# SSD scan: x and B turned on VectorE in blocks of 32 and carried through DRAM, and the within-chunk products of two chunks in one block

## The chip, the cores and the metric

The kernel runs on one core of a Trainium2 chip. The metric is the device time of that core for one execution, in microseconds (us); a kernel's time is the median of several runs. The engines are named as the profile names them: PE is TensorE (matmuls and transposes, with PEld for its weight loads), DVE is VectorE, ACT is ScalarE, POOL is GpSimd, and SP is the engine whose queue issues most of the transfers.

## The reference

One layer of a hybrid decoder on a sequence of S = 512 tokens with D = 1024 channels: a projection feeds a state-space mixer (SSD) and a sliding-window attention, both are merged and projected, and a SwiGLU network follows. The change lies in the SSD part alone. Cut to that part, with 4 groups of 8 heads, a head of 64 channels, a state of 128 and chunks of T = 128 tokens (names shortened):

```python
X  = (xh * dt[..., None])                      # chunk, T, group, head, 64
a_cum = cumsum(dt * a, over the chunk)
Lmat = exp(segsum(dt * a))                     # lower triangle
CB = einsum('bclgn,bcsgn->bcgls', Cc, Bc)
y_diag = einsum('bcgels,bcsgep->bclgep', Lmat * CB, X)          # within a chunk
states = einsum('bclgn,bcgel,bclgep->bcgepn', Bc, decay, X)     # what a chunk leaves
h_in   = scan over chunks: h * exp(a_cum[-1]) + states
y_off  = einsum('bclgn,bcgepn,bcgel->bclgep', Cc, h_in, exp(a_cum))
y = y_diag + y_off + d_skip * xh
y = y * silu(z);  y = y * rsqrt(mean over the group of y*y) * w  # grouped norm
```

Before it, x, B and C come from the projection by a causal convolution over four tokens and a SiLU.

## The kernel before

Activations lie with channels on the partitions and tokens along the row. So x of one group is four tiles `xs_f` of 128 channels x 512 tokens (two heads each), B and C are a tile `bc_f` each, and y of a group is `y_g`, four such tiles side by side.

*Products.* A product of the layer's weights is made in float32 precision from halves: `mm3` (L149 to L151) issues three matmuls, high x high, high x low and low x high, for each of eight slices of 128 channels, thus 24 matmuls of 128x512 into one PSUM tile `ps_mm`. A unit is such a product with its 512 KB of weights. The class `Units` loads a unit's weights into `w_raw` (four buffers, on SP's queue, L120), ACT makes the high half `w_hi` (L135) and DVE the low half `w_lo` (L136), three units ahead of the product.

*The scan.* There are 16 steps, i = 4g + c, for group g and chunk c. A step needs matmuls that depend on each other through DVE, ACT and POOL, and between them PE works on units that wait in a list, the *filler*; `fill(6.0)` issues matmuls of the list in threes until 6.0 us of them are used, and so 27 or 30 matmuls. The filler's units are the x, B, C of the next group (`x`, with the convolution of `g_xbc`: ACT L368, three DVE operations named `cacc`, L371, and the SiLU), the z of this one (`z`) and, from group 1 on, products of the layer's end. In threes of matmuls, group 0 has 80 of them, groups 1 and 2 have 112, and group 3 has 128; the slots of a group ask for some 110. Where the list is empty `fill` issues nothing; `all_done(prefix)` issues what is left of the units of that name.

The parts of a step:
- `ssd_pre(i)`: loads `L` (the cumulated sums of one group of heads, spread over 128 partitions, 512 KB) and `E` on SP, POOL masks `L` (L754), ACT puts the exponential on its eight tiles (L759). `L` has three buffers.
- `ssd_a(i)`: PE makes `ps_cb` = B C (L774), DVE multiplies `L` by it (L778, "L*cb" below). PE transposes the chunk of x, four passes into `ps_x` (L781), DVE multiplies by dt into `X` (L784). For chunks 0 to 2 PE also transposes B (`ps_bt`, L790), ACT copies it to `bt`, and POOL makes `Xd` = X times the decay (L795). For c = 0 ACT first puts D*x into `y_g`.
- `ssd_b(i)`: PE makes `ps_st` from `Xd` and `bt` (L809), the new state `h_st` follows on POOL and DVE; PE makes `ps_yo` (L825), what the state gives, DVE multiplies it by `E` to `yo`, and POOL adds that to `y_g`. After a stretch of filler PE makes `ps_yd`, from `X` and `L`, eight matmuls for the eight heads, which the profile counts as sixteen passes (L834), and DVE adds it to `y_g` (L836).
- `gate_norm(g)`, once a group is done: DVE multiplies `y_g` by z (L850), ACT squares, POOL adds up the squares (L856), ACT and DVE make the halves `sqr` (L231), PE sums over the partitions (`ps_ms`, L863), and DVE takes a reciprocal (L865).

*Who sets the order.* PE's order is the order of the code, by hand (`manual_schedule`). The instructions of the other engines are put in order by the framework's scheduler; the PSUM tiles of the scan (`ps_cb`, `ps_x`, `ps_bt`, `ps_st`, `ps_yo`, `ps_yd`) share five buffers, and those of the filler have three of their own. Each queue issues in its order: a transfer on SP that waits holds all behind it.

The functions and the loop around the change, with the profile's line numbers:

Of the kernel before, what the change touches and what calls it, by code (L numbers as in the profile page):

```python
# [11 lines left out]
F32 = mybir.dt.float32  # L12
# [50 lines left out]
def kernel(  # L63
# [89 lines left out]
    class Filler:  # L153
# [115 lines left out]
    def axt(shape, name):  # L269
        return psX.tile(shape, F32, name=name, tag="ax")  # L270
# [463 lines left out]

    z_t, y_t, yn_t, L_t, E_t, a_t, h_t = {}, {}, {}, {}, {}, {}, {}

    def ssd_pre(i):
# [19 lines left out]
        for j in range(2):  # L757
            for t in range(4):
                nc.scalar.activation(L[:, j, t], L[:, j, t], AF.Exp, bias=nac5[:, g, j, c, t:t + 1], scale=1.0)  # L759

    def ssd_a(i):

# [15 lines left out]
        nc.vector.tensor_tensor(out=Lf, in0=Lf, in1=cb.unsqueeze(1).broadcast_to([P, 8, P]), op=ALU.mult)  # L778
        ps = axt([P, 4, 2, 64], "ps_x")
        for t in range(4):  # L780
            nc.tensor.transpose(ps[:, t].rearrange("p j d -> p (j d)"), xs[t][:, cs], ident)  # L781
        X = sd.tile([P, 4, 2, 64], F32, name="X", tag="X", bufs=2)
        for j in range(2):
            nc.vector.tensor_tensor(  # L784
                out=X[:, :, j], in0=ps[:, :, j],
                in1=dt5[:, g, j, c].unsqueeze(2).broadcast_to([P, 4, 64]), op=ALU.mult)
        bt = Xd = None
        if c < NT - 1:
            ps = axt([P, P], "ps_bt")
            nc.tensor.transpose(ps, b_f[:, cs], ident)  # L790
            bt = sd.tile([P, P], F32, name="bt", tag="bt", bufs=2)
            nc.scalar.copy(out=bt, in_=ps)
            Xd = sd.tile([P, 4, 2, 64], F32, name="Xd", tag="Xd", bufs=2)
            for j in range(2):
                nc.gpsimd.tensor_tensor(  # L795
                    out=Xd[:, :, j], in0=X[:, :, j],
                    in1=dec5[:, g, j, c].unsqueeze(2).broadcast_to([P, 4, 64]), op=ALU.mult)
        a_t[i] = (X, bt, Xd)

    def ssd_b(i):  # L800

        g, c = divmod(i, NT)
        cs = slice(c * P, (c + 1) * P)
        y, c_f, L = y_t[g], xbc_t[g, 1], L_t.pop(i)
        X, bt, Xd = a_t.pop(i)
        h_prev = h_t.pop(g, None)
        if c < NT - 1:
            pss = axt([P, 4, 2, 64], "ps_st")
            nc.tensor.matmul(  # L809
                pss.rearrange("p t j d -> p (t j d)"), bt, Xd.rearrange("p t j d -> p (t j d)"),  # L810
                start=True, stop=True)
# [18 lines left out]
        yield  # L830
        psd = axt([P, 4, P], "ps_yd")
        for t in range(4):
            for j in range(2):
                nc.tensor.matmul(  # L834
                    psd[64 * j:64 * j + 64, t], X[:, t, j], L[:, j, t], start=True, stop=True)
        nc.vector.tensor_add(y[:, :, cs], y[:, :, cs], psd)  # L836
        yield
# [432 lines left out]
```

## Time and profile before

| what | value |
|---|---|
| median of 3 runs | 1028.93 us (1028.39 to 1028.96) |
| the profiled execution | 1028.11 us, of which the span is 1026.2 us |
| DVE, ACT, POOL busy | 600.5, 505.8 and 205.5 us (59%, 49%, 20%) |
| transfers | 126.56 MB, 123 GB/s over the span |
| the chain that ended last | 86% PE, 4% DVE, 3% ACT, 3% DMA |
| weights `w_raw` | 187 transfers of 512 KB, 3.5 us each to landing |
| `L` | 16 transfers of 512 KB, 5.4 us each to landing |

The span is what the profiler sees from the first instruction to the last; the execution's time is longer by what lies around it. All edits of this change lie in the scan, which runs from about 237 to 580 us of the span.

### The profile page before, as it was taken

To read this page: it belongs to the slowest core of one execution; us is meant where nothing else is said; L and a number is where in the kernel's file an instruction comes from. 1 tells how busy PE (TensorE), PEld (TensorE's weight loads), DVE (VectorE), ACT (ScalarE), POOL (GpSimd) and SP (SyncE) were. 2 spreads that over 40 slices of the span, in tenths; PEclk is the share of its full clock that TensorE was granted. 3 is DMA by queue.
4 is the path that set the end of the run, shared out by engine and by line. 5 is a ranking of instruction groups with operands and counts; after the bars stand their busy time and mean duration, and the time that the engine had idled before them with its cause. 6 is when DMAs were issued, how large, how long until landed. Compare 5 with 4: busy or idle time off the path is not lost.

```text
span 1026.2 us, 13200 instructions
## 1 busy us (share of the span) xinstructions
PE 1014.5 (99%) x5044; PEld 837.6 (82%) x5044; DVE 600.5 (59%) x835; ACT 505.8 (49%) x864; POOL 205.5 (20%) x195
## 2 busy tenths in 40 slices
PE   9999999999999999999999999999999999999997
PEld 7888888887887878888888888898888888888886
DVE  6789874534656764676664595646433333332765
ACT  6464566717666885783733542434332333322450
POOL 2011223723115113111223820390000000000000
PEclk9999999999999999999999999999999999999999
DMA  8211223544443334334322344316433333331471
GB/s 317 83 64 61 88 83 104 203 142 130 136 135 106 113 116 126 106 115 138 89 93 82 123 150 179 102 42 225 144 123 123 106 120 106 120 123 62 154 255 43
DMA packets 38799, 126.56 MB, mean 123 GB/s; under 512 B 4528, under 2 KB 5040, under 8 KB 38480
## 3 DMA queue, kind: packets, MB, share of 16 engines
q1 hardware_dynamic: 36080, 116.14, 34.7%
q0 software_dynamic: 2080, 7.47, 2.0%
q10 hardware_dynamic: 576, 2.10, 0.6%
q8 instruction: 40, 0.66, 0.2%
q14 instruction: 23, 0.19, 0.1%
HBM read 119.27 MB, written 6.42 MB: 122 GB/s over the span
## 4 chain that ended last, share of the span: by engine, by line
PE 86%; DVE 4%; ACT 3%; DMA 3%; issue 2%; POOL 1%; SPq 0%; DVEq 0%; POOLq 0%; ACTq 0%
PE ps_mm L149 13%; PE ps_mm L150 12%; PE ps_mm L151 12%; PE ps_ff L151 8%; PE ps_ff L149 8%; PE ps_ff L150 8%; PE ps_da L151 2%; PE ps_da L149 2%; PE ps_da L150 2%; DMA L<-a_d 2%; PE ps_db L151 2%; PE ps_db L150 2%; PE ps_db L149 2%; PE ps_mix L149 1%; PE ps_mix L151 1%
## 5 line engine op out<-in xcount | busy, mean ns | idle before, releaser
L135 ACT CAST w_hi<-w_raw 128x1024 fp32r<-128x1024 f32 x185 | 193.4, 1051 | 305.5 <-PE ps_ff L150 123.2
L136 DVE TENSOR_TENSOR w_lo<-w_raw,w_hi 128x1024 fp32r<-128x1024 f32 x185 | 240.5, 1305 | 154.1 <-ACT w_hi L135 151.9
L149 PE MATMUL ps_mm<-hT_hi,w_hi 128*128 128x512 f32 x504 | 203.3, 403 | 1.0 <-DVE cacc L371 1.0
L150 PE MATMUL ps_mm<-hT_lo,w_hi 128*128 128x512 f32 x504 | 196.8, 391 | 0.0
L151 PE MATMUL ps_mm<-hT_hi,w_lo 128*128 128x512 f32 x504 | 196.6, 390 | 0.0
L149 PE MATMUL ps_ff<-h2T_hi,w_hi 128*128 128x512 f32 (+1 forms) x384 | 143.2, 373 | 0.0
L150 PE MATMUL ps_ff<-h2T_lo,w_hi 128*128 128x512 f32 (+1 forms) x384 | 142.6, 371 | 0.0
L151 PE MATMUL ps_ff<-h2T_hi,w_lo 128*128 128x512 f32 (+1 forms) x384 | 142.6, 371 | 0.0
L149 PEld LDWEIGHTS ps_mm<-hT_hi,w_hi 128*128 128x128 f32 x504 | 94.7, 188 | 23.1 <-issue 5.6
L151 PEld LDWEIGHTS ps_mm<-hT_hi,w_lo 128*128 128x128 f32 x504 | 94.6, 188 | 20.3
L150 PEld LDWEIGHTS ps_mm<-hT_lo,w_hi 128*128 128x128 f32 x504 | 94.8, 188 | 18.2 <-issue 1.0
L150 PEld LDWEIGHTS ps_ff<-h2T_lo,w_hi 128*128 128x128 f32 x384 | 72.3, 188 | 12.6
L151 PEld LDWEIGHTS ps_ff<-h2T_hi,w_lo 128*128 128x128 f32 x384 | 72.3, 188 | 12.5
L149 PEld LDWEIGHTS ps_ff<-h2T_hi,w_hi 128*128 128x128 f32 x384 | 72.3, 188 | 12.4
L1117 DVE TENSOR_TENSOR sgf<-sgf,ps_ff 128x512 f32<-128x512 f32 x22 | 15.1, 685 | 68.4 <-PE ps_ff L151 68.4
L149 PE MATMUL ps_mm<-yh,w_hi 128*128 128x512 f32 x124 | 49.2, 397 | 0.0
L150 PE MATMUL ps_mm<-yl,w_hi 128*128 128x512 f32 x124 | 48.3, 390 | 0.0
L151 PE MATMUL ps_mm<-yh,w_lo 128*128 128x512 f32 x124 | 48.3, 389 | 0.0
L371 DVE SCALAR_TENSOR_TENSOR cacc<-ps_mm,pc,cacc 128x511 f32<-128x511 f32 (+2 forms) x54 | 39.9, 741 | 9.8 <-ACT cacc L368 9.2
L759 ACT ACTIVATE L<-L,nac 128x128 f32<-128x128 f32 x128 | 40.9, 391 | 6.2 <-POOL L L754 5.9
L778 DVE TENSOR_TENSOR L<-L,cb 128x1024 f32<-128x1024 f32 x16 | 21.5, 1343 | 38.4 <-ACT cb L776 21.6
L754 POOL TENSOR_SCALAR_AFFINE_SELECT L<-L 128x1024 f32<-128x1024 f32 x16 | 20.1, 1256 | 93.9 <-DMA L<-a_d 93.9
(267 smaller groups left out, 1700.2 us busy)
## 6 DMA issues: line engine op xcount, KB each, us to landing
w_raw<-in_wall_dram SPq DMA_DIRECT2D x187, 512.0 KB, 3.5
L<-a_d SPq DMA_DIRECT2D x16, 512.0 KB, 5.4
E<-e_d SPq DMA_DIRECT2D x24, 128.0 KB, 3.5
x_d<-x_sb POOLq DMA_DIRECT2D x4, 512.0 KB, 7.8
row<-x_d POOLq DMA_DIRECT2D x4, 512.0 KB, 5.1
h_d<-row POOLq DMA_DIRECT2D x4, 512.0 KB, 3.0
h_r<-h_d ACTq DMA_DIRECT2D x4, 512.0 KB, 5.4
out_dram<-y_o SPq DMA_DIRECT2D x7, 256.0 KB, 4.1
```

What stands on the lines that cost most here:

```text
L135: (copy or nc.scalar.copy)(out=hi, in_=w)
L136: self.last = (eng or nc.vector).tensor_sub(out=lo, in0=w, in1=hi.bitcast(F32))
L149: nc.tensor.matmul(ps, lh, rh, start=start, stop=False)
L150: nc.tensor.matmul(ps, lh, rl, start=False, stop=False)
L151: nc.tensor.matmul(ps, ll, rh, start=False, stop=stop)
L371: nc.vector.scalar_tensor_tensor(out=acc[:, d:], in0=ps[:, :S - d], scalar=pc[:, cw + 3 - d:cw + 4 - d], in1=acc[:, d:], op0=ALU.mult, op1 ...
L754: nc.gpsimd.affine_select(out=Lf, in_=Lf, pattern=[[0, 8], [1, P]], compare_op=ALU.is_ge, fill=-BIG, base=0, channel_multiplier=-1)
L759: nc.scalar.activation(L[:, j, t], L[:, j, t], AF.Exp, bias=nac5[:, g, j, c, t:t + 1], scale=1.0)
L778: nc.vector.tensor_tensor(out=Lf, in0=Lf, in1=cb.unsqueeze(1).broadcast_to([P, 8, P]), op=ALU.mult)
L1117: nc.vector.tensor_mul(sg, sg, pu)
```

## The change

The transposes leave PE. A new `ssd_x(i)` turns the chunk of x on DVE: one instruction turns each 32x32 block of a 128x128 piece by itself, so that the blocks still stand in their old places; four of them write `T`. The blocks are moved to their places through DRAM: one store `T` to `t_d` (SP), and four loads to `R`, each for 32 partitions (pieces of 512 bytes). For chunks 0 to 2 it does the same with B: one transpose to `Tb`, one store to `b_d`, four loads to `bt` (pieces of 128 bytes). A new `ssd_dt(i)` makes `X` = R times dt on DVE and `Xd` on POOL. `ssd_a` keeps D*x, `ps_cb` and L*cb, and loses its five transposes, ACT's copy and the rest. `ssd_x` stands two steps ahead, `ssd_dt` one. `ssd_b` makes `ps_yd` only at even chunks, for that chunk and the next in one block of 32 passes into two PSUM tiles, and both additions to `y_g` follow. `all_done` for the next group's x moves from chunk 3 to chunk 2. `T` shares three buffers with other temporaries, `R`, `Tb` and `Xd` have one each (`Xd` had two), `X` and `bt` keep two.

```diff
--- before.py
+++ after.py
@@ -234,6 +234,8 @@
     h_d = dram.tile([S, D], F32, name="h_d")
     a_d = dram.tile([P, P], F32, name="a_d")
     e_d = dram.tile([P, P], F32, name="e_d")
+    t_d = dram.tile([NG * NT, P, 4, P], F32, name="t_d")
+    b_d = dram.tile([NG * NT, P, 4, 32], F32, name="b_d")
 
 
     def xbc(g):
@@ -732,7 +734,7 @@
     er = e_d.rearrange("(g j c t) l -> g c j (t l)", g=NG, j=2, c=NT)
     dt5, dec5, cd5, nac5 = cols(dtv), cols(dec), cols(cdec), cols(nac)
 
...
 
     def ssd_pre(i):
 
@@ -758,6 +760,52 @@
             for t in range(4):
                 nc.scalar.activation(L[:, j, t], L[:, j, t], AF.Exp, bias=nac5[:, g, j, c, t:t + 1], scale=1.0)
 
+    def ssd_x(i):
+
+        g, c = divmod(i, NT)
+        cs = slice(c * P, (c + 1) * P)
+
+        T = sd.tile([P, 4, 4, 32], F32, name="T", tag="tmp", bufs=3)
+        for t in range(4):
+            nc.vector.transpose(T[:, :, t], xbc_t[g, 2 + t][:, cs])
+
+        R = sd.tile([P, 4, 4, 32], F32, name="R", tag="R", bufs=1)
+        R_t[i] = R
+        nc.sync.dma_start(out=t_d[i], in_=T.rearrange("p b t s -> p b (t s)"))
+        for b in range(4):
+            nc.sync.dma_start(
+                out=R[32 * b:32 * b + 32].rearrange("r a t s -> r a (t s)"),
+                in_=t_d[i, :, b].rearrange("(a r) x -> r a x", r=32))
+        if c < NT - 1:
+            Tb = sd.tile([P, P], F32, name="Tb", tag="Tb", bufs=1)
+            nc.vector.transpose(Tb, xbc_t[g, 0][:, cs])
+            bt = sd.tile([P, P], F32, name="bt", tag="bt", bufs=2)
+            bt_t[i] = bt
+            nc.sync.dma_start(out=b_d[i], in_=Tb.rearrange("p (b s) -> p b s", b=4))
+            for b in range(4):
+                nc.sync.dma_start(
+                    out=bt[32 * b:32 * b + 32].rearrange("r (a s) -> r a s", a=4),
+                    in_=b_d[i, :, b].rearrange("(a r) s -> r a s", r=32))
+
+    def ssd_dt(i):
+
+        g, c = divmod(i, NT)
+        R = R_t.pop(i)
+        X = sd.tile([P, 4, 2, 64], F32, name="X", tag="X", bufs=2)
+        X_t[i] = X
+        for j in range(2):
+            nc.vector.tensor_tensor(
+                out=X[:, :, j].rearrange("p t (h s) -> p t h s", h=2),
+                in0=R[:, 2 * j:2 * j + 2].rearrange("p h t s -> p t h s"),
+                in1=dt5[:, g, j, c].unsqueeze(2).unsqueeze(3).broadcast_to([P, 4, 2, 32]), op=ALU.mult)
+        if c < NT - 1:
+            Xd = sd.tile([P, 4, 2, 64], F32, name="Xd", tag="Xd", bufs=1)
+            Xd_t[i] = Xd
+            for j in range(2):
+                nc.gpsimd.tensor_tensor(
+                    out=Xd[:, :, j], in0=X[:, :, j],
+                    in1=dec5[:, g, j, c].unsqueeze(2).broadcast_to([P, 4, 64]), op=ALU.mult)
+
     def ssd_a(i):
 
         g, c = divmod(i, NT)
@@ -776,38 +824,17 @@
         nc.scalar.copy(out=cb, in_=ps)
         Lf = L.rearrange("p j t l -> p (j t) l")
         nc.vector.tensor_tensor(out=Lf, in0=Lf, in1=cb.unsqueeze(1).broadcast_to([P, 8, P]), op=ALU.mult)
-        ps = axt([P, 4, 2, 64], "ps_x")
-        for t in range(4):
-            nc.tensor.transpose(ps[:, t].rearrange("p j d -> p (j d)"), xs[t][:, cs], ident)
-        X = sd.tile([P, 4, 2, 64], F32, name="X", tag="X", bufs=2)
-        for j in range(2):
-            nc.vector.tensor_tensor(
-                out=X[:, :, j], in0=ps[:, :, j],
-                in1=dt5[:, g, j, c].unsqueeze(2).broadcast_to([P, 4, 64]), op=ALU.mult)
-        bt = Xd = None
-        if c < NT - 1:
-            ps = axt([P, P], "ps_bt")
-            nc.tensor.transpose(ps, b_f[:, cs], ident)
-            bt = sd.tile([P, P], F32, name="bt", tag="bt", bufs=2)
-            nc.scalar.copy(out=bt, in_=ps)
-            Xd = sd.tile([P, 4, 2, 64], F32, name="Xd", tag="Xd", bufs=2)
-            for j in range(2):
-                nc.gpsimd.tensor_tensor(
-                    out=Xd[:, :, j], in0=X[:, :, j],
-                    in1=dec5[:, g, j, c].unsqueeze(2).broadcast_to([P, 4, 64]), op=ALU.mult)
-        a_t[i] = (X, bt, Xd)
 
     def ssd_b(i):
 
         g, c = divmod(i, NT)
         cs = slice(c * P, (c + 1) * P)
-        y, c_f, L = y_t[g], xbc_t[g, 1], L_t.pop(i)
-        X, bt, Xd = a_t.pop(i)
+        y, c_f = y_t[g], xbc_t[g, 1]
         h_prev = h_t.pop(g, None)
         if c < NT - 1:
             pss = axt([P, 4, 2, 64], "ps_st")
             nc.tensor.matmul(
-                pss.rearrange("p t j d -> p (t j d)"), bt, Xd.rearrange("p t j d -> p (t j d)"),
+                pss.rearrange("p t j d -> p (t j d)"), bt_t.pop(i), Xd_t.pop(i).rearrange("p t j d -> p (t j d)"),
                 start=True, stop=True)
             h = sd.tile([P, 4, 2, 64], F32, name="h_st", tag="h_st", bufs=2)
             h_t[g] = h
@@ -828,12 +855,19 @@
             nc.vector.tensor_mul(yo, pso, E_t.pop(i))
             nc.gpsimd.tensor_add(y[:, :, cs], y[:, :, cs], yo)
         yield
-        psd = axt([P, 4, P], "ps_yd")
-        for t in range(4):
-            for j in range(2):
-                nc.tensor.matmul(
-                    psd[64 * j:64 * j + 64, t], X[:, t, j], L[:, j, t], start=True, stop=True)
-        nc.vector.tensor_add(y[:, :, cs], y[:, :, cs], psd)
+
+        if c % 2 == 0:
+            psd = [axt([P, 4, P], "ps_yd") for _ in range(2)]
+            for k in range(2):
+                X, L = X_t.pop(i + k), L_t.pop(i + k)
+                for t in range(4):
+                    for j in range(2):
+                        nc.tensor.matmul(
+                            psd[k][64 * j:64 * j + 64, t], X[:, t, j], L[:, j, t],
+                            start=True, stop=True)
+            for k in range(2):
+                cs = slice((c + k) * P, (c + k + 1) * P)
+                nc.vector.tensor_add(y[:, :, cs], y[:, :, cs], psd[k])
         yield
 
     def g_z(g, t):
@@ -938,8 +972,11 @@
 
     ssd_pre(0)
     ssd_pre(1)
+    ssd_x(0)
     ssd_a(0)
     fill(4.0)
+    ssd_dt(0)
+    ssd_x(1)
     norm = iter(())
     for i in range(NG * NT):
         g, c = divmod(i, NT)
@@ -952,12 +989,16 @@
         if i + 2 < NG * NT:
             ssd_pre(i + 2)
         if i + 1 < NG * NT:
-            if c == NT - 1:
-                all_done(f"x{g + 1}")
             ssd_a(i + 1)
         fill(f0)
         b = ssd_b(i)
         next(b)
+        if i + 1 < NG * NT:
+            ssd_dt(i + 1)
+        if i + 2 < NG * NT:
+            if c == NT - 2:
+                all_done(f"x{g + 1}")
+            ssd_x(i + 2)
 
         slots = (0, 1, 1) if g == NG - 1 else (2, 3, 4)
         fill(f1)
```

What it does to the order is shown at three places. A number behind a name tells one tile from another.

The first is DVE where the scan starts. Before, X_2243 and X_2279 are the X of chunks 0 and 1, made from PE's `ps_x`, and L_2199 and L_2212 are their L:

```order
L414 TENSOR_TENSOR tB_639<-tB_639,ps_mm_2159 128x512
L784 TENSOR_TENSOR X_2243<-ps_x_2238,dtv_95 128x4x64 x2
L136 TENSOR_TENSOR w_lo_2294<-w_raw_2096,w_hi_2293 128x1024
L784 TENSOR_TENSOR X_2279<-ps_x_2274,dtv_95 128x4x64 x2
L778 TENSOR_TENSOR L_2199<-L_2199,cb_2235 128x1024
L778 TENSOR_TENSOR L_2212<-L_2212,cb_2271 128x1024
L371 SCALAR_TENSOR_TENSOR cacc_2321<-ps_mm_2290,pc_79,cacc_2321 128x511
L371 SCALAR_TENSOR_TENSOR cacc_2321<-ps_mm_2290,pc_79,cacc_2321 128x510
```

After, X_2259 and X_2361 are the X of chunks 0 and 1, T_2367 is the turned x of chunk 2, and Tb_2276 and Tb_2378 are the turned B of chunks 1 and 2; the T of chunks 0 and 1 stand ahead of these rows:

```order
L770 STREAM_TRANSPOSE T_2367<-xs_f_943 128x4x32
L770 STREAM_TRANSPOSE T_2367<-xs_f_1094 128x4x32
L770 STREAM_TRANSPOSE T_2367<-xs_f_1251 128x4x32
L770 STREAM_TRANSPOSE T_2367<-xs_f_1393 128x4x32
L781 STREAM_TRANSPOSE Tb_2276<-bc_f_612 128x128
L826 TENSOR_TENSOR L_2201<-L_2201,cb_2256 128x1024
L826 TENSOR_TENSOR L_2214<-L_2214,cb_2302 128x1024
L373 SCALAR_TENSOR_TENSOR cacc_2337<-ps_mm_2306,pc_79,cacc_2337 128x511
L136 TENSOR_TENSOR w_lo_2348<-w_raw_2130,w_hi_2347 128x1024
L797 TENSOR_TENSOR X_2259<-R_2235,dtv_97 128x4x64 x2
L373 SCALAR_TENSOR_TENSOR cacc_2337<-ps_mm_2306,pc_79,cacc_2337 128x510
L373 SCALAR_TENSOR_TENSOR cacc_2337<-ps_mm_2306,pc_79,cacc_2337 128x509
```

X(0) stood ahead of both L*cb, next to them, and now stands behind them, with T(2) and Tb(1) ahead of L*cb and a `cacc` and a `w_lo` behind.

The second is SP's queue at the same place. Before, only L, E and weights:

```order
L120 DMA w_raw_2291<-in_wall_dram 128x1024
L743 DMA L_2199<-a_d_82 128x2x512
L743 DMA L_2212<-a_d_82 128x2x512
L750 DMA E_2214<-e_d_83 64x512 x2
L743 DMA L_2253<-a_d_82 128x2x512
L750 DMA E_2255<-e_d_83 64x512 x2
L120 DMA w_raw_2329<-in_wall_dram 128x1024
```

After, with T_2230 and T_2265 those of chunks 0 and 1, and R_2235 and bt_2243 what comes back for chunk 0:

```order
L745 DMA L_2201<-a_d_82 128x2x512
L745 DMA L_2214<-a_d_82 128x2x512
L752 DMA E_2216<-e_d_83 64x512 x2
L774 DMA t_d_84<-T_2230 128x512
L784 DMA b_d_85<-Tb_2241 128x128
L774 DMA t_d_84<-T_2265 128x512
L745 DMA L_2284<-a_d_82 128x2x512
L776 DMA R_2235<-t_d_84 32x4x128 x4
L786 DMA bt_2243<-b_d_85 32x4x32 x4
L784 DMA b_d_85<-Tb_2276 128x128
L752 DMA E_2286<-e_d_83 64x512
```

The stores of T(0), Tb(0) and T(1) stand ahead of the third L, and the loads of R(0) and bt(0) behind it.

The third is DVE where group 0 ends and group 1 has begun. Before, the `y_g` rows with z are the first part of gate_norm(0), X_2877 is X(5) and L_2773 is L(5):

```order
L784 TENSOR_TENSOR X_2877<-ps_x_2872,dtv_95 128x4x64
L850 TENSOR_TENSOR y_g_2228<-y_g_2228,z_2622 128x512
L850 TENSOR_TENSOR y_g_2228<-y_g_2228,z_2681 128x512
L850 TENSOR_TENSOR y_g_2228<-y_g_2228,z_2728 128x512
L850 TENSOR_TENSOR y_g_2228<-y_g_2228,z_2771 128x512
L778 TENSOR_TENSOR L_2773<-L_2773,cb_2869 128x1024
L784 TENSOR_TENSOR X_2877<-ps_x_2872,dtv_95 128x4x64
L231 TENSOR_TENSOR sqr_2848<-sq_2832,sqr_2847 128x512
L371 SCALAR_TENSOR_TENSOR cacc_2919<-ps_mm_2888,pc_79,cacc_2919 128x511
```

After, X_2995 is X(5), L_2667 and L_2840 are L(4) and L(5), and T_3001 is the turned x of chunk 6:

```order
L884 TENSOR_TENSOR y_g_2249<-y_g_2249,z_2838 128x512
L826 TENSOR_TENSOR L_2667<-L_2667,cb_2863 128x1024
L231 TENSOR_TENSOR sqr_2915<-sq_2899,sqr_2914 128x512
L770 STREAM_TRANSPOSE T_3001<-xs_f_2410 128x4x32
L770 STREAM_TRANSPOSE T_3001<-xs_f_2468 128x4x32
L770 STREAM_TRANSPOSE T_3001<-xs_f_2527 128x4x32
L770 STREAM_TRANSPOSE T_3001<-xs_f_2596 128x4x32
L826 TENSOR_TENSOR L_2840<-L_2840,cb_2936 128x1024
L373 SCALAR_TENSOR_TENSOR cacc_2971<-ps_mm_2940,pc_79,cacc_2971 128x511
L136 TENSOR_TENSOR w_lo_2982<-w_raw_2719,w_hi_2981 128x1024
L373 SCALAR_TENSOR_TENSOR cacc_2971<-ps_mm_2940,pc_79,cacc_2971 128x510
L797 TENSOR_TENSOR X_2995<-R_2885,dtv_97 128x4x64
```

X(5) was half ahead of the norm's y*z and half behind it; it now stands behind the norm's `sqr`, the transposes of chunk 6 and L*cb(5), among the convolution and a weight's low half.

More of the change, by code (lines that the diff above doesn't have):

```diff
@@ L733 @@
     dt5, dec5, cd5, nac5 = cols(dtv), cols(dec), cols(cdec), cols(nac)
-    z_t, y_t, yn_t, L_t, E_t, a_t, h_t = {}, {}, {}, {}, {}, {}, {}
+    z_t, y_t, yn_t, L_t, E_t, R_t, X_t, Xd_t, bt_t, h_t = ({} for _ in range(10))
     def ssd_pre(i):
```

## The prediction

> **What bounds the kernel now.** I read the engines' share of the span first, then the busy time by stretch.
>
> ```profile
> span 1026.2 us, 13200 instructions
> PE 1014.5 (99%) x5044; PEld 837.6 (82%) x5044; DVE 600.5 (59%) x835; ACT 505.8 (49%) x864; POOL 205.5 (20%) x195
> ```
> ```profile
> 237.00:340.00 103.00, 101.79 (x531) 82.05 (x530) 62.90 (x76) 73.90 (x136) 33.91 (x32) 1.00 0.44 125
> ...
> 500.00:580.00 80.00, 80.00 (x411) 65.04 (x410) 47.22 (x52) 36.62 (x53) 27.64 (x21) 1.00 0.28 90
> ```
>
> The columns are length, then PE, PE's weight loads, DVE, ACT and POOL, then clock, DMA share and GB/s. The scan runs from 237 to about 580 us. In its first stretch PE stands idle for 1.2 us, in its last not at all. So PE work taken out is worth its whole time; and PE's order is written by hand, so a wait on PE costs its whole length, since nothing later on PE can make it up. The longest wait in the scan today:
>
> ```profile
> PE ps_mm L149 <- DVE cacc L371: 1.0, 1, 1.0
> ```
>
> **What leaves PE.** The transposes, and the edges of eight blocks:
>
> ```profile
> L781 PE MATMUL ps_x<-ident,xs_f 128*128 128x128 f32 x64 | 9.6, 273 | 0.0
> ```
> ```profile
> 237.00 0.60 PE L781 MATMUL ps_x<-ident,xs_f 128*128 128x128 f32 x4
> ...
> 367.50 0.39 PE L150 MATMUL ps_mm<-hT_lo,w_hi 128*128 128x512 f32 x1
> 367.73 0.39 PE L151 MATMUL ps_mm<-hT_hi,w_lo 128*128 128x512 f32 x1
> 368.05 1.09 PE L834 MATMUL ps_yd<-L,X 128*64 128x128 f32 x16
> 369.07 0.50 PE L149 MATMUL ps_mm<-hT_hi,w_hi 128*128 128x512 f32 x1
> 369.41 0.40 PE L150 MATMUL ps_mm<-hT_lo,w_hi 128*128 128x512 f32 x1
> ```
>
> Matmuls overlap in the pipeline, so the price is the pitch and not the busy time. Four ps_x in 0.60 us, each 0.273 long, are (0.60-0.273)/3 = 0.109 us apart. 64 of x and 12 of B at 0.109: **-8.3 us**. A ps_yd block: from the ps_mm at 367.73 to the second ps_mm after it are 1.68 us, of which two ps_mm are 0.46 (pitch 0.23), so the block costs 1.22. Its sixteen passes are (1.09-0.273)/15 = 0.0545 apart, 0.87 in all; the other 0.35 is entering and leaving it. Sixteen blocks become eight: 8 x 0.35 = **-2.8 us**. Together -11.1.
>
> **What the new route costs off PE.** No row shows a DVE transpose. It is bounded by the shortest 128x128 float32 operation on DVE and by the reciprocal, the slowest per element (3349/512 x 128 = 840 ns).
>
> ```profile
> L439 DVE COPY_PREDICATED ps_sc<-beyond,ps_sc 128x128 f32<-128x128 int32 x16 | 4.6, 289 | 3.7 <-PE ps_sc L434 3.6
> ```
> ```profile
> L865 DVE RECIPROCAL sq<-sq 128x512 f32<-128x512 f32 x4 | 13.4, 3349 | 5.5 <-ACT sq L864 5.5
> ```
> ```profile
> L371 DVE SCALAR_TENSOR_TENSOR cacc<-ps_mm,pc,cacc 128x511 f32<-128x511 f32 x18 | 13.2, 735 | 9.2 <-ACT cacc L368 9.2
> ```
> ```profile
> L136 DVE TENSOR_TENSOR w_lo<-w_raw,w_hi 128x1024 fp32r<-128x1024 f32 x185 | 240.5, 1305 | 154.1 <-ACT w_hi L135 151.9
> ```
>
> I take 0.29, since a transpose moves its data once as the copy does: 76 x 0.29 = 22 us of DVE, over 340 us in which it is some 60% busy; by 0.84 it is 64 us. Spread out, either is hidden under PE; in two places it is not. The twelve bt copies that ACT loses, and the multiplication by dt that reads R in SBUF instead of PSUM, come to nothing on PE.
>
> The Trainium skill, "VectorE: DVE Perf Modes", in "The three transpose paths" puts a 128x128 bf16 transpose on DVE at 311 ns, in separate blocks of 32, and its rules for authors send a 128x128 transpose to TensorE where PSUM will do as a destination. By its figure the DVE work would be an estimated 23.6 us, and by its rule the change goes the wrong way; the pitch of 0.109 above agrees that PE does it cheaply.
>
> **Place one: the start.** ps_st(0) needs Xd(0) and bt(0). Before, PE made both on the spot. Now their way is DVE, a store, loads, DVE and POOL, and PE has the same thirty ps_mm to fill it.
>
> ```profile
> 237.92 2.08 SPq L750 DMA_DIRECT2D E<-e_d  x2
> 240.04 0.98 SPq L743 DMA_DIRECT2D L<-a_d  x1
> ```
> ```profile
> 244.66 1.09 POOL L754 TENSOR_SCALAR_AFFINE_SELECT L<-L 128x1024 f32<-128x1024 f32 x1 [0.96 <-DMA L<-a_d]
> 248.15 1.09 POOL L754 TENSOR_SCALAR_AFFINE_SELECT L<-L 128x1024 f32<-128x1024 f32 x1 [2.40 <-DMA L<-a_d]
> ```
> ```profile
> 243.24 4.99 ACT L759 ACTIVATE L<-L,nac 128x128 f32<-128x128 f32 x16
> ```
> ```profile
> 248.32 2.00 DVE L778 TENSOR_TENSOR L<-L,cb 128x1024 f32<-128x1024 f32 x1 [1.31 <-ACT L L759]
> ```
> ```profile
> 236.78 0.38 PE L774 MATMUL ps_cb<-bc_f 128*128 128x128 f32 x2
> ...
> 238.66 0.48 PE L149 MATMUL ps_mm<-hT_hi,w_hi 128*128 128x512 f32 x1
> ...
> 245.60 0.59 PE L809 MATMUL ps_st<-Xd,bt 128*128 128x512 f32 x1
> ```
>
> PE asks for ps_st 6.94 us after the filler starts. With the transposes gone the filler starts two cb (four passes of 0.109) after 236.78: 237.2 + 6.9 = 244.2. Two chains bring the operands, and X(0) needs both.
> - By DMA: SP is busy with L and E until 240.0 and stores T(0) then. L(1) landed at 244.6 and L(2) at 248.1; between them lie two E and one L, 0.75 MB in 3.5 us, first come first served. By that rate the E land at 245.8, T(0) at 247.0; then Tb(0), T(1) and L(2), 0.8 MB, go first, and R(0) lands at 250.9 + 1.2 = 252.1, bt(0) about 253.
> - On DVE, in its order: Tb(1) waits for the store of Tb(0) (247.3), with both L*cb queued behind it; L*cb(1) waits for ACT's exponentials (243.24 + 4.99 = 248.2) and ends between 249.6 and 250.3. Then come a cacc (0.74) and a w_lo (1.3), and only then X(0): 252.3 at the latest.
>
> X(0) at 252.3; the two halves of X at 0.4 and of Xd at 0.7, overlapped, take 1.8: 254.1. PE waits 9.9 us, say **+10**. From below 9.2 (the faster L*cb); from above 13 (14 transposes of 0.84 ahead of L*cb).
>
> After such a gap PE is slow. The first transposes of the run and its end show how:
>
> ```profile
> 1.53 7.04 PE L545 MATMUL ps_warm<-ident 128*128 128x128 f32 x40 [1.53 <-POOL ident masks.py:199]
> ...
> 8.52 4.09 PE L545 MATMUL ps_warm<-ident 128*128 128x128 f32 x36
> ```
> ```profile
> 1018.00:1020.00 2.00, 0.82 (x7) 0.61 (x6) 1.07 (x3) 0.00 (x0) 0.00 (x0) 1.00 0.00 0
> ...
> 1024.00:1026.00 2.00, 0.00 (x0) 0.00 (x0) 0.00 (x0) 0.00 (x0) 0.00 (x0) 0.50 0.19 66
> ```
>
> Forty passes took 7.04 us; at the later pitch (4.09/36) it is 4.5. The clock is at 0.50 some 5 us after the last matmul, and 10 us is twice that: **+2.5**, from below 0.
>
> **Place two: from group 0 to group 1.** Here group 0 has no filler left, and DVE and POOL hold gate_norm(0). ps_yd(5) now stands in the block of ps_yd(4), a chunk earlier, and needs X(5), which DVE issues behind that norm. Count from the end of ps_yd(2,3). PE arrives after 18 ps_mm (4.1), cb, yo, cb (twelve passes, 1.3), 30 ps_mm (6.9), st (two passes of four times the columns, 0.9), 27 ps_mm (6.2) and ps_yd(4) (1.0): 20.4 us.
>
> ```profile
> 306.47 2.02 POOL L754 TENSOR_SCALAR_AFFINE_SELECT L<-L 128x1024 f32<-128x1024 f32 x1 [9.19 <-DMA L<-a_d]
> ...
> 314.49 5.66 POOL L856 TENSOR_TENSOR sq<-sq,s 128x512 f32<-128x512 f32 x3
> ```
> ```profile
> 311.86 4.90 DVE L850 TENSOR_TENSOR y_g<-y_g,z 128x512 f32<-128x512 f32 x4
> ```
>
> The other side: L(5) and L(6), whose buffers ps_yd(2) and (3) free, land about 4.3 and 6.7 after that point (L(2) above took 8.1 from issue, with more ahead of it); POOL masks both (2.0 each, to 8.7) and only then adds yo(3) (1.3): 10.0. y*z, 4.9: 14.9. POOL's sums of squares, 5.7, begin after the second square: 18.8. sqr on ACT and DVE: 20.1; T(6) 1.2; L*cb(5), after ACT's other exponentials, ends at 23; three cacc, a w_lo and X(5) in turn: 27. With uncontended durations it is 24.3. So a wait of 3.9 to 6.6, say 5.3; the 1.0 of before at this place goes: **+4.3**. From below -1.0, if the wait is covered.
>
> In later groups all slots have filler: from yo(7) to ps_yd(8,9) stand 114 ps_mm, 26 us, against 27 - 5.4 = 22 for the same chain from yo on: no wait. SP gets ten transfers more in a chunk of 20 us, at 0.45 each (two L in 0.90), and R's loads wait on it for the X before; but weights are loaded four units ahead (4 x 24 x 0.23 = 22 us), which hides that.
>
> **Sum.** -8.3 - 2.8 + 10 + 2.5 + 4.3 = +5.7, on a profiled execution of 1028.1 us: 1033.8. The median of the runs shown is 0.8 above that execution: **1034.6**.
>
> **Rivals.**
> - *The second wait is covered*: -11.1 + 10 + 2.5 - 1.0 = +0.4, 1029.3. For it: every engine but PE runs on for 10 us at the start. Against it: the chain above starts from ps_yd(2,3), so a head start does not shorten it.
> - *The clock falls in the second gap too*: another 2.5, 1037.1. For it: that gap is as long as the fall took at the end; against it, it may just end before. The Trainium skill, "TensorE: Matmul & The Clock Gate", Part 1, halves the clock after an idle window of about 3.4 us and frees it after as much steady work; by that the two restarts would cost an estimated 1.7 each, 1035.5 in all.
> - *The round trip overlaps* (faster): the gap at ps_st(0) stays at its lower end with the clock up, and the idle time there covers the second place: -11.1 + 9.2 - 1.0 = -2.9, 1026.0. It decides from a loss on PE, waits and slow clock together, under 9 us. For it: no row in the scan shows the clock falling. Against it: DVE's order puts X(0) last whatever the DMA does.
> - *SP's queue becomes the bound*: R late by 2 to 3 us at each of eight blocks, +16 to +20 on top of -11.1 + 10 + 0 to 2.5: 1044 to 1050. Against it: a DMA share of 0.28 to 0.44 in the scan.
>
> **Chances.** 0.2% (2 us) is about what a measurement of this kernel can tell from no change. The forecast 0.43 (1031 to 1040), clock in both gaps 0.12, covered second wait 0.20 (nearly all of it the same), overlap 0.17 (most of it faster), queue 0.08. Faster 0.18, same 0.18, slower 0.64. The range takes in the overlap and ends at the queue's lower end: 1025 to 1045.
>
> **What would show it.** PE's waits name ps_st <- POOL Xd for some 10 us near 244 and ps_yd for about 5 near 320; the pitch of ps_mm doubles for a few us after the first; DVE's transposes are near 0.29; ps_yd comes in eight blocks of 2.1 us. I am wrong if ps_st waits under 7 us, if PE waits in the later groups, or if a transpose takes over 0.5.

## The result, and the profile after

The changed kernel takes 1033.48 us (median of 5 runs, 1033.07 to 1034.26), beside 1028.86 us for the kernel before (5 runs): a ratio of 1.0053, 95% interval 1.0042 to 1.0064. The medians lie 4.6 us apart, and the ratio stands for 5.5 us; gains given below "by the ratios" against the changed kernel come out about 1 us smaller by the medians. The profiled execution, 1034.26 us with a span of 1032.6 us, is the longest of the five. The page and the two stretches of the scan that were shown of before:

```profile
span 1032.6 us, 13369 instructions
PE 1008.3 (98%) x4968; PEld 833.3 (81%) x4968; DVE 619.7 (60%) x911; ACT 496.0 (48%) x845; POOL 207.7 (20%) x195
```
```profile
237.00:340.00 103.00, 89.12 (x448) 71.21 (x447) 62.99 (x107) 62.78 (x116) 26.83 (x29) 0.92 0.54 161
500.00:580.00 80.00, 80.00 (x408) 65.29 (x407) 49.37 (x56) 37.24 (x53) 28.00 (x23) 1.00 0.35 106
```

PE is busy for 6.2 us less, and is idle for 13.9 us of the first stretch (1.2 before), where its mean clock is 0.92. In the last stretch it is never idle, and the transfers there have become more without being felt. PE's waits, total, times and longest:

```profile
PE ps_st L836 <- POOL Xd L805: 9.7, 1, 9.7
PE ps_yd L865 <- DVE X L797: 4.2, 2, 3.9
```

These are the two places. The first, by the timelines of SP, DVE and PE (start, length, instruction, and in brackets the idle time ahead with what ended it):

```profile
240.42 0.91 SPq L774 DMA_DIRECT2D t_d<-T  x1
...
246.94 1.75 SPq L776 DMA_DIRECT2D R<-t_d  x4
```
```profile
247.17 0.31 DVE L781 STREAM_TRANSPOSE Tb<-bc_f 128x128 f32<-128x128 f32 x1 [5.38 <-DMA b_d<-Tb]
247.41 1.18 DVE L826 TENSOR_TENSOR L<-L,cb 128x1024 f32<-128x1024 f32 x1
249.24 1.22 DVE L826 TENSOR_TENSOR L<-L,cb 128x1024 f32<-128x1024 f32 x1 [0.66 <-issue]
250.39 0.74 DVE L373 SCALAR_TENSOR_TENSOR cacc<-ps_mm,pc,cacc 128x511 f32<-128x511 f32 x1
251.05 1.55 DVE L136 TENSOR_TENSOR w_lo<-w_raw,w_hi 128x1024 fp32r<-128x1024 f32 x1
252.52 0.75 DVE L797 TENSOR_TENSOR X<-R,dtv 128x256 f32<-128x256 f32 x2
```
```profile
254.37 2.07 PE L836 MATMUL ps_st<-Xd,bt 128*128 128x512 f32 x2 [9.71 <-POOL Xd L805]
```

The store of T(0) is issued at 240.42, and SP can issue the loads that wait for it only at 246.94: 6.5 us for 256 KB behind 1.25 MB of L and E. Meanwhile DVE stands at Tb(1), which waits for the store of Tb(0) to free its buffer (a second buffer for Tb was not tried). Then both L*cb, a convolution step and a low half pass ahead of X(0).

The second place, at the change from group 0 to group 1, on DVE and PE:

```profile
327.30 0.69 DVE L231 TENSOR_TENSOR sqr<-sq,sqr 128x512 fp32r<-128x512 f32 x1 [3.21 <-ACT sqr L230]
327.91 0.89 DVE L770 STREAM_TRANSPOSE T<-xs_f 128x128 f32<-128x128 f32 x4
328.92 1.23 DVE L826 TENSOR_TENSOR L<-L,cb 128x1024 f32<-128x1024 f32 x1
330.06 0.74 DVE L373 SCALAR_TENSOR_TENSOR cacc<-ps_mm,pc,cacc 128x511 f32<-128x511 f32 x1
330.72 1.22 DVE L136 TENSOR_TENSOR w_lo<-w_raw,w_hi 128x1024 fp32r<-128x1024 f32 x1
331.85 0.74 DVE L373 SCALAR_TENSOR_TENSOR cacc<-ps_mm,pc,cacc 128x510 f32<-128x510 f32 x1
332.51 0.75 DVE L797 TENSOR_TENSOR X<-R,dtv 128x256 f32<-128x256 f32 x1
```
```profile
328.52 1.09 PE L865 MATMUL ps_yd<-L,X 128*64 128x128 f32 x16
333.52 0.66 PE L865 MATMUL ps_yd<-L,X 128*64 128x128 f32 x2 [3.90 <-DVE X L797]
```

DVE is idle for 3.2 us ahead of the norm's `sqr` with X(5) queued behind it, and then does five other things first: the transposes of chunk 6, L*cb(5), two convolution steps and a low half. The loads of R(5) had been issued from 321.78 on and had landed by 325.1. PE, done with ps_yd(4) at 329.6, stands until 333.5. Behind both waits the clock is at half (it is the third column from the right; the windows are cut where it changes, and `...` stands for windows left out):

```profile
244.71:248.12 3.41, 0.00 (x0) 0.00 (x0) 0.95 (x2) 2.84 (x10) 1.09 (x1) 1.00 0.92 276
248.12:251.53 3.41, 0.00 (x0) 0.00 (x0) 2.75 (x4) 2.63 (x6) 1.09 (x1) 0.50 0.65 138
...
254.94:258.36 3.42, 3.42 (x7) 1.99 (x6) 0.76 (x2) 2.24 (x3) 1.10 (x2) 0.50 0.31 74
258.36:261.77 3.41, 3.41 (x16) 2.79 (x15) 0.00 (x0) 0.42 (x1) 1.24 (x3) 1.00 0.95 215
...
330.04:333.45 3.41, 0.00 (x0) 0.00 (x0) 3.41 (x6) 2.56 (x4) 1.97 (x3) 1.00 0.30 83
333.45:336.86 3.41, 3.08 (x17) 2.36 (x18) 3.41 (x6) 1.91 (x2) 1.18 (x2) 0.50 0.52 179
336.86:340.28 3.42, 3.42 (x9) 2.65 (x8) 1.50 (x4) 0.63 (x1) 0.00 (x0) 0.50 0.96 261
340.28:343.69 3.41, 3.41 (x16) 2.82 (x15) 0.96 (x1) 1.73 (x2) 1.17 (x2) 1.00 0.73 213
```

A DVE transpose takes what the copy of that size took before (busy time, mean in ns):

```profile
L770 DVE STREAM_TRANSPOSE T<-xs_f 128x128 f32<-128x128 f32 x64 | 14.5, 277 | 0.1
```

Below, each block of other work between the filler's matmuls is priced by what it puts off: the time from the last filler matmul ahead of it to the last of the up to sixteen behind it, less 0.2267 us (the filler's pitch) for each.

### The profile page after: what moved, and what is told of

It reads as the page before. It is cut to its first block, busy times and chain, and to the rows that moved or that the text cites. A ratio compares the mean times of both kernels' runs of the same rounds, so it can differ in the third digit from the quotient of the medians.

```text
span 1032.6 us, 13369 instructions
## 1 busy us (share of the span) xinstructions
PE 1008.3 (98%) x4968; PEld 833.3 (81%) x4968; DVE 619.7 (60%) x911; ACT 496.0 (48%) x845; POOL 207.7 (20%) x195
## 4 chain that ended last, share of the span: by engine, by line
PE 93%; DVE 3%; DMA 2%; issue 1%; ACT 1%; POOL 1%; SPq 0%; DVEq 0%; POOLq 0%
PE ps_mm L149 15%; PE ps_mm L150 14%; PE ps_mm L151 14%; PE ps_ff L149 8%; PE ps_ff L151 8%; PE ps_ff L150 8%; PE ps_da L149 2%; PE ps_da L151 2%; PE ps_da L150 2%; PE ps_db L151 2%; PE ps_db L150 2%; PE ps_db L149 2%; PE ps_yd L865 1%; PE ps_mix L149 1%; PE ps_mix L150 1%; PE ps_mix L151 1%
## 5 line engine op out<-in xcount | busy, mean ns | idle before, releaser
L136 DVE TENSOR_TENSOR w_lo<-w_raw,w_hi 128x1024 fp32r<-128x1024 f32 x185 | 244.3, 1324 | 181.7 <-ACT w_hi L135 179.5
L856 POOL TENSOR_TENSOR y_g<-y_g,yo 128x512 f32<-128x512 f32 x12 | 15.5, 1295 | 98.9 <-ACT y_g L819 55.8
```

What stands on the lines that cost most here:

```text
L136: self.last = (eng or nc.vector).tensor_sub(out=lo, in0=w, in1=hi.bitcast(F32))
L856: nc.gpsimd.tensor_add(y[:, :, cs], y[:, :, cs], yo)
```

## The experiments

The theory: the work taken off PE is worth its 11 us, and two places, each a matter of what is queued ahead of an operand, cost more than that. The main rival: the new route is dear as such, in DVE time, transfers or SP's queue, wherever it stands. All changes of time are against the kernel before on the same chip.

**The start: chunks 0 and 1 on PE again.**

```diff
-    ssd_x(0)
     ssd_a(0)
+    ssd_pe(0)       # ps_x, X, ps_bt, bt, Xd as before the change
     fill(4.0)
-    ssd_dt(0)
-    ssd_x(1)
...
+            ssd_pe(1)   # in step 0, in place of ssd_dt(1)
```

> The changed kernel, but chunks 0 and 1 get X, bt and Xd by transposes on PE as before the change; the other fourteen keep the new route. Theory 1 (the wait at the first ps_st and the slow clock behind it are the start's whole cost): 9.7 + 2.2 us go, ten transposes come back at about 0.11 (1.1), so 1033.5 - 10.8 = 1022.7, and up to 3.6 less if the second gap happens to miss the clock's fall (1019 to 1023). PE has no wait over 1 us before 300 us. Rival (the transfers and the DVE work of the new route are what costs, wherever they first stand): the wait comes back at ps_yd(0,1), ps_st(1) or ps_st(2), and the gain is under 5, thus above 1028.5.

1022.38 us, ratio 0.9945 (0.9933 to 0.9957): 5.5 us faster than before, and by the two ratios 1.1% or 11 us faster than the changed kernel. Its clock is at 1.00 until 321.8, and the only wait over 1 us in the scan is the second place's (2.9 and 0.5, with 3.5 of slow clock). So two chunks out of sixteen carried the whole loss at the start, and the other fourteen round trips did not.

**The second place: X(5) ahead of the norm.** `ssd_dt` is split in its DVE and its POOL half:

```diff
...
+        if i == 4:
+            ssd_dt(5)           # DVE half
         if c == 0 and g > 0:
             norm = gate_norm(g - 1)
...
-            ssd_dt(i + 1)
+            if i != 4:
+                ssd_dt(i + 1)
+            ssd_dec(i + 1)      # POOL half: Xd
```

> The changed kernel with the multiplication that makes X(5) written ahead of gate_norm(0); on DVE it then stands right behind L*cb(5), ahead of two convolution steps and a low half of weights that stood before it. Theory 1 (place on DVE sets the wait): X(5) ends about 2.4 us earlier, PE waits about 1.3 instead of 3.9 + 0.3, too short for the clock to fall: 1033.5 - 2.9 - 3.6 = 1027.0. Rival A (L*cb(5) or R(5) sets it): wait and time as in the changed kernel, 1033 to 1034. Rival B (the wait shrinks, but the slow clock comes with any wait): 1030.6.

1027.46 us, ratio 0.9996 (0.9987 to 1.0005): 0.6% less than the changed kernel, by the ratios 5.9 us. The wait is 0.6, not 1.3 (X(5) starts at 329.44, right behind L*cb(5)), and the clock stays up. Theory 1 holds: the place of two instructions of 0.4 us each was worth 6 us, and by the profiles 3.6 of it came through the clock.

**The second place: chunks 4 and 5 not paired.**

```diff
-        if c % 2 == 0:
-            psd = [axt([P, 4, P], "ps_yd") for _ in range(2)]
+        n = 1 if i in (4, 5) else 2
+        if c % n == 0:
+            psd = [axt([P, 4, P], "ps_yd") for _ in range(n)]
...
```

> The changed kernel, but chunks 4 and 5 have a ps_yd block each; the other six pairs stay. Theory 1 (X(5) is late only because pairing asks for it a chunk early): the waits of 3.9 and 0.3 and the slow clock behind them (3.6) go, an edge comes back (0.4), the old wait of about 1 at ps_yd(4) or (5) may return: 1033.5 - 7.4 = 1026.1, to 1027.1. Rival (gate_norm(0) holds DVE and POOL and whatever stands behind it on PE waits, paired or not): a wait of 3 or more stays at ps_yd(4), ps_yo(5) or ps_yd(5), 1030.5 or more.

1029.51 us, ratio 1.0014 (1.0004 to 1.0023): 4.0 us better than the changed kernel by the ratios, where 6.4 to 7.4 were expected. In its profile the wait at ps_yd is gone, its clock falls only at the start, and ps_yd(4) costs 2.2 instead of 1.25, which is the old wait of 1.0. So the mechanism is as expected. Its profile shows where most of the missing time went. Level with the changed kernel's at the first ps_yd (263.5), it has saved 6.3 us at the ps_cb behind the second place (359.72, against 366.02). Then 1.3 are lost in the next stretch of filler, at a wait that the changed kernel does not have, and 0.3 at a ps_yo:

```profile
366.66 0.50 PE L149 MATMUL ps_mm<-hT_hi,w_hi 128*128 128x512 f32 x1 [1.07 <-ACT z L877]
```

That leaves the 4.7 by which the two spans differ; the profiled execution of the changed kernel is 0.8 longer than its median. Moving X(5) is the better repair.

**The parts alone.** First the pairing, on the kernel before; `ps_x` and `ps_bt` stay:

```diff
-        psd = axt([P, 4, P], "ps_yd")
+        if c % 2 == 0:
+            psd = [axt([P, 4, P], "ps_yd") for _ in range(2)]
```

> The kernel before with the pairing of ps_yd alone; all transposes stay on PE. Theory 1: eight block edges less, 8 x 0.38 = 3.0, and X(5), which here needs neither store nor load, is in time: 1028.9 - 3.0 = 1025.9 (to 1024.9 if the old wait of 1.0 goes). Rival (pairing alone makes the second wait, since it asks for X(5) and L(5) while the norm holds DVE): a wait of 3 to 5 at ps_yd(5) with up to 3.6 of slow clock, 1029 to 1034.

1029.61 us, ratio 1.0009 (1.0000 to 1.0017). Neither the theory's time nor the rival's wait: there is no wait at ps_yd(5), the edges are saved, and yet it is no faster. One chunk later stands a wait that nobody had named, with the clock behind it:

```profile
PE ps_yo L825 <- ACT cb L776: 2.3, 1, 2.3
...
PE ps_bt L790 <- DVE yo L828: 1.1, 1, 1.1
```
```profile
337.12:340.53 3.41, 1.08 (x8) 0.88 (x8) 0.90 (x1) 3.39 (x7) 0.00 (x0) 1.00 0.00 0
340.53:343.94 3.41, 3.41 (x11) 2.73 (x10) 3.41 (x6) 3.19 (x9) 0.00 (x0) 0.50 0.12 20
343.94:347.35 3.41, 3.41 (x16) 2.78 (x16) 2.44 (x3) 3.06 (x4) 1.19 (x2) 1.00 0.57 175
```

`ps_yo` does not read `cb`. What it shares with `ps_cb` is the five PSUM tiles of the scan, and ACT's copy that empties `ps_cb` stands behind eight exponentials, the last of them behind a SiLU and two ACT_TABLE_LOADs of 1.28 us each. The paired `ps_yd` holds one tile more, and the new route holds two fewer (`ps_x`, `ps_bt`). That the two halves of the change help each other in this way is an inference from the names in the waits; no run with more PSUM tiles was made. The eleven runs spread from 1027.08 to 1030.66: four take up to 1028.30 at a mean clock of 0.997 or 0.998, the other seven 1029.13 and more at 0.995 to 0.997, the profiled one among them. That suggests that the slow clock behind this wait does not come in every run; no profile of the faster four was kept.

Then the new route, with a `ps_yd` block for each chunk (n = 1 throughout):

> The new route for x and B alone: ps_yd has a block per chunk as before the change. Theory 1: -8.0 (the 76 transposes) + 9.6 (wait at the start) + 2.5 (slow clock) and no second wait beyond the 1 to 2 that the kernel before has: +3 to +4 against the kernel before. Rival (the second wait comes from the route, not from pairing): a wait of 3 or more at ps_yd(4) or ps_yd(5), +7 to +10.

1031.4 us, ratio 1.0031 (1.0020 to 1.0041), +3.2 us, as expected. The start waits 9.6; at ps_yd(4) and (5) no wait is listed, only the old one of a ps_mm for `cacc`, now 1.2. The second place needs both halves: the route, which puts X(5) behind the norm, and the pairing, which asks for it a chunk early.

**Both repairs together:** chunks 0 and 1 on PE, and X(5) ahead of the norm.

> Both repairs together: chunks 0 and 1 by transposes on PE, and X(5) written ahead of gate_norm(0). Theory 1 (the two places are separate and add): against the kernel before -5.5 (chunks 0 and 1 on PE, as measured) and another -6 from the second place, whose wait and slow clock stayed in that run (3.4 + 3.5): -11 to -12, a ratio of 0.989, and no clock below 1.00 between the warm-up and the end. Rival (a repair of one place only shifts the wait to a later group, since the chain after it runs earlier): -6 to -8.

1016.33 us (1016.07 to 1016.82), ratio 0.9886 (0.9871 to 0.9901): 11.7 us faster than before and, by the ratios, 17 us faster than the changed kernel. The longest wait on PE in the scan is 0.7, and the clock is at 1.00 from 4.35 to 1011.28 us. The two places add. With fourteen chunks on the new route the gain is about what the work taken off PE was to bring, so nothing of size is left of the rival.

**How much of the start is order.** All chunks on the new route, X(5) ahead of the norm, and chunk 0's part written ahead of the loads of L (the cut is against the run with X(5) ahead):

```diff
+    ssd_x(0)
+    ssd_dt(0)
+    ssd_dec(0)
     ssd_pre(0)
     ssd_pre(1)
-    ssd_x(0)
     ssd_a(0)
     fill(4.0)
-    ssd_dt(0)
-    ssd_dec(0)
     ssd_x(1)
```

> The changed kernel with X(5) ahead of the norm, and with all of chunk 0's new route written ahead of the loads of L: on SP the store of T(0) then stands behind one L instead of two L and two E, and the loads of R(0) ahead of E; on DVE X(0) stands behind one L*cb instead of two, a cacc and a w_lo. All chunks keep the new route. Theory 1 (of the 9.7 some 6.5 are the store behind 1.25 MB of loads and 1.8 the place on DVE): R(0) lands near 246, X(0) ends at 248.3, Xd(0) at 249.5: a wait of about 5 instead of 9.5, -4 to -5 against the kernel before. Rival A (the round trip itself takes as long whatever stands ahead): a wait of 8 to 10, 0 to -1. Rival B (the L that are put back now hold the first ps_yd): a wait of 3 or more there, -1 to -3.

1022.64 us, ratio 0.9946 (0.9933 to 0.9958): 5.6 us faster than before. The wait is 4.1:

```profile
239.11 0.33 SPq L774 DMA_DIRECT2D t_d<-T  x1
...
241.15 1.75 SPq L776 DMA_DIRECT2D R<-t_d  x4
```
```profile
246.91 0.93 DVE L797 TENSOR_TENSOR X<-R,dtv 128x256 f32<-128x256 f32 x2 [0.64 <-DMA R<-t_d]
```

The same store of 256 KB takes 2.0 us instead of 6.5, with a single L ahead of it that was issued at 234.7. What is left of the wait is now the loads of R(0): issued from 241.15 on, behind a second L issued at 240.02, they keep X(0) until 246.91. At the second place a wait of 1.9 at ps_yd, with slow clock behind it, is back although X(5) is written ahead of the norm: DVE stands 3.6 us for `sqr` there, and X(5) starts at 324.89, later than PE asks for it. So the kernel is faster than before even with every transpose off PE, if the order is right, but X(5) moved alone does not always cover the second place.

**One chunk on PE, the other not.** Chunk 0 on PE, chunk 1 by the new route, X(5) ahead of the norm:

> As the run with both repairs, but only chunk 0 on PE; chunk 1 goes by the new route from the start, with R free for it at once. Theory 1 (the start is a matter of latency: X(1) is asked for some 15 us after the scan begins, and its way, store at 240.4, loads from 247, behind two L*cb, ends at 250.5 to 252.5): PE waits 0 to 1 at the first ps_yd, and five transposes (0.5) are saved: -0.5 to +0.5 against the run with both repairs. Rival (DVE's or SP's queue carries chunk 1 later than that): a wait of 2 or more there, with slow clock 4 or more.

1023.45 us, ratio 0.9956 (0.9944 to 0.9968), 7 us more than both repairs: a miss, but not for the rival's reason. X(1) ends at 250.7 and the first ps_yd does not wait. PE waits 5.0 at ps_st(0), where the list of waits names POOL, which was long done. The late operand is bt(0), on ACT:

```profile
246.18 2.44 ACT L761 ACTIVATE L<-L,nac 128x128 f32<-128x128 f32 x8 [0.30 <-POOL L L756]
249.00 0.69 ACT L761 ACTIVATE L<-L,nac 128x128 f32<-128x128 f32 x2 [0.38 <-POOL L L756]
249.60 0.24 ACT L832 COPY bt<-ps_bt 128x128 f32<-128x128 f32 x1
```

The scheduler had put a copy of 0.24 us behind eighteen exponentials. With chunk 0's transposes written ahead of `ps_cb` (and `ssd_x(1)`, which stood ahead of `ssd_a(0)`, behind `fill(4.0)` as in the changed kernel):

> The run with only chunk 0 on PE, with one thing mended: the transposes of chunk 0 are written ahead of ps_cb, so that ACT copies bt(0) at once and not behind eighteen exponentials. Theory 1 (in the run before, that copy alone held ps_st(0): it ended at 249.8, Xd(0) at 241.4 and X(1) at 250.7): no wait at ps_st(0), X(1) ends at 250.5 to 252.5 and PE waits 0 to 1 at the first ps_yd: the time of the run with both repairs, -11 to -12.5 against the kernel before. Rival (chunk 1 by the new route is too late as well, hidden in that run by PE's own wait of 5.0): a wait of 2 or more at the first ps_yd and slow clock, -6 to -9.

1018.83 us, ratio 0.9908 (0.9895 to 0.9922), -9.5. At the start no wait is left. The place of `ssd_x(1)` hardly mattered to that (T(1) is stored at 240.25 instead of 240.14), and the copy of bt(0) now ends at 238.2, so the copy was the cause. But at the second place there are waits of 1.6 (ps_st) and 1.3 (ps_yd), where both repairs together have only one of 0.7 (ps_yd). The result lies between the two expectations, and the rival's wait stands in another place than it said. DVE's row shows one step of it: three of the four transposes of T(4) stand behind two low halves, its store goes out at 294.53 instead of 291.54, and X(4) is made from 305.63 on instead of 298.52. Why the order there changes with one chunk more on the new route is open.

**The clock by itself.** Transposes of the identity fill the waits, into tiles that the real matmuls overwrite:

```diff
+            if i == 0:
+                for _ in range(76):
+                    nc.tensor.transpose(pss[:, 0].rearrange("p j d -> p (j d)"), ident, ident)
...
+                if i + k == 5:
+                    for _ in range(26):
+                        nc.tensor.transpose(psd[k][:, 0], ident, ident)
```

> The changed kernel with 76 further transposes of the identity on PE ahead of the first ps_st (some 8.6 us) and 26 between ps_yd(4) and ps_yd(5) (2.9 us), into PSUM tiles that the real matmuls overwrite: they fill most of the two waits with work that nobody uses. Theory 1 (the clock is taken down by PE's idle time): the operands come at the same moments, the clock stays at 1.00 through both places, and 2.2 + 3.6 = 5.8 go: against the kernel before -1 to 0, a ratio of about 0.999. Rival (the slow matmuls behind the waits have another cause, such as the transfers that then run): the same time as the changed kernel, +4 to +5.

1032.91 us (1029.65 to 1034.53), ratio 1.0039 (1.0024 to 1.0055), in two groups. Three of seven runs, the profiled one among them, take 1029.65 to 1030.15 at a mean clock of 0.998, and its trace shows 1.00 through both places; the other four take 1032.91 to 1034.53 at 0.995 or 0.996. Even the three are about 2 us above the kernel before, where 0 to 1 below it was expected; in the profile PE still waits 1.4, 0.9 and 0.7 around the fillings. With 92 and 42 instead:

> The changed kernel with 92 and 42 filling transposes instead of 76 and 26, so that PE has work until the operands are there (10.4 and 4.7 us against waits of 9.7 and 4.2). Theory 1 (idle PE takes the clock down, and the runs of the former try that came out 3 to 4 us longer, at a mean clock of 0.995 instead of 0.998, had lost it in what was left of a wait): no slow clock in any run, 0 to +2 against the kernel before (2.0 of it for filling longer than the wait and for edges), and a spread under 2. Rival (the filling transposes do not hold the clock reliably): two groups of runs again, some 3 us apart.

1033.83 us, ratio 1.0056 (1.0043 to 1.0068). The mean clock is 0.998 or 0.999 in all five runs, so idle PE is what takes it down. Yet the time is that of the changed kernel: by the blocks up to 363 us it has lost 3.9 us less, and then PE waits for ACT in group 1 (`yacc` 1.7, `z` 1.0), where the changed kernel does not: from the ps_cb at 362.83 to the ps_yd at 424.28 it takes 61.5 us, against 57.6 for the same stretch there. So with a higher clock alone the time was lost again later. In the run with chunks 4 and 5 not paired part of the gain went the same way (1.3 at a wait for ACT); with X(5) moved it did not.

## Why the prediction was right, point by point

| term | predicted | in the profiles |
|---|---|---|
| 76 transposes | -8.3 | -8.0 |
| 8 edges of ps_yd | -2.8 | -3.0 |
| wait at ps_st(0) | +10 | +9.7 |
| slow clock behind it | +2.5 | +2.2 |
| wait at ps_yd(5), less the 1.0 of before | +5.3 - 1.0 | +4.2 - 1.1 |
| slow clock behind that | 0 | +3.6 |
| other small waits of before | 0 | -1.4 |
| sum | +5.7 | +6.2 |

- *What leaves PE.* The price by the pitch holds: the 1.25 of a single ps_yd block twice becomes 2.12, and a block of ps_cb with its transposes goes from 0.80 (without B 0.67) to 0.27.
- *The start.* The moments came as worked out: SP's loads at 246.94 against a store that was to land at 247.0, X(0) at 252.52 against 252.3, ps_st at 254.37 against 254.1. DVE's order did put X(0) last, R(0) having landed at 251.2, some 0.9 earlier than worked out. But "whatever the DMA does" was too strong, since that order itself stood 5.4 us for a transfer, the store of Tb(0). With the store of T(0) behind one L and X(0) behind one L*cb, the wait fell to 4.1.
- *The second place.* Right in cause, 1.1 too long; both lie in the stated 3.9 to 6.6.
- *The step that failed* is the clock in the second gap. The forecast had it end before the fall, by "some 5 us after the last matmul"; it was left to a rival at 0.12. The fall came at 333.45, as PE resumed, and cost 3.6, more than behind the long gap and more than the 2.5 at which the rival had priced it. It was offset by the shorter wait and by 1.4 of small waits of before (0.5 at the start, 0.2 and 0.7 at two `ps_yo`) that the sum had left standing. So the closeness of 1034.6 to 1033.48 is in part luck. Between the medians lie 4.6, since the profiled run of the changed kernel is 0.8 above its median and that of the kernel before 0.75 below.
- *The page's rule.* The Trainium skill, "VectorE: DVE Perf Modes", in its rules for kernel authors, sends a 128x128 transpose to TensorE where PSUM will do as its destination. The changed kernel as it stands seems to agree; but with the two places mended and fourteen chunks still on DVE the kernel is 11.7 us faster than before. About 3 of that are the edges. What the route alone is worth no run shows; with all chunks on it and no pairing the kernel was 3.2 slower, with 9.6 of wait and 1.6 of slow clock at the start, which leaves an estimate of -8.0. So here, where PE is the bound, the measurements go against the rule. A float32 block transpose took 277 ns, the forecast's 0.29.
- *The rivals.* A covered second wait and the overlap did not come; SP's queue did not bind, with no PE wait over 1 us in later groups.

## What to carry to other kernels

When operands move from the engine that is the bound to a longer way round, the price is not the work but the first use and every place where the lead is lost. Here, in the best order, 14 of 16 chunks were free, and two places had cost 20 us (9.7 + 2.2 + 4.2 + 3.6). Before judging such a change, look at what is queued ahead of the new store and of the operand's last instruction, and whether a buffer with one copy makes an engine stand with others behind it. Repair the wait, not what follows it: with the waits filled and the clock up in all five runs, the time here was still that of the changed kernel.

## What the runs showed of the hardware

The clock is decided in fixed windows. Between the warm-up and the end of each trace its low spells last 3.413, 6.827 or 10.240 us (1, 2 and 3 times 3.413), and within each run the later changes stand at whole multiples of it after the first (in the changed kernel 242.346 = 71 x 3.413, 75.093 = 22 x 3.413). It fell behind windows in which PE was busy for 0.00 to 0.44 of the time and stayed up behind those with 0.51 and more (PE's ends are modelled by the profiler, so the shares are not exact):

```profile
323.63:327.04 3.41, 1.49 (x19) 1.29 (x18) 3.41 (x6) 3.41 (x5) 1.58 (x3) 1.00 0.00 0
327.04:330.45 3.41, 3.41 (x9) 2.62 (x9) 3.41 (x9) 1.35 (x2) 1.78 (x2) 0.50 0.46 156
```
```profile
407.59:411.00 3.41, 1.75 (x9) 1.31 (x8) 2.26 (x5) 2.91 (x5) 0.47 (x1) 1.00 0.01 2
411.00:414.41 3.41, 3.41 (x16) 2.82 (x15) 3.28 (x6) 1.23 (x3) 0.00 (x0) 1.00 0.66 186
```

The first pair is of the run with chunk 0 written early (a wait of 1.9 in one window, and the clock fell), the second of the run with 92 and 42 fillings (0.51, and it stayed). So a wait of 2 us costs at least half of 3.4 us more if it falls into one window (1.9, by the blocks, behind the wait of 2.3 with the pairing alone), and by the same rule, an estimate that no profile shows, nothing more if it is split by two; the two groups of runs with the pairing alone would fit that. What brings the clock back is not settled: it rose behind windows that were busy for 0.83 (the new route without pairing) and 0.88 (chunk 0 early), and stayed low for another behind 0.85 (chunks 0 and 1 on PE) and 0.90 (the changed kernel), which is why behind the waits of 3.4 and 4.2 us there the slow clock cost 3.5 and 3.6. The Trainium skill, "TensorE: Matmul & The Clock Gate", Part 1, gives a free-running window of 3413 ns; the runs agree. It asks for an idle window, where here 0.44 busy was idle enough. Where the windows lie differs between executions: the first rise came between 4.3 and 7.5 us.
